# Routing's heads on VectorE, query weights in own buffers, x ahead of the second weight, attention's mask as one product

## The chip, the core and the metric

The kernel runs on one core of a Trainium2 chip. The metric is the device time of one execution in microseconds, taken as the median of several; before the change it is 4402.1 us, the median of 3 runs from 4399.16 to 4411.26 us. The core's engines work side by side, each in the order of its own queue: TensorE (PE in the profile, its weight loads PEld), VectorE (DVE), ScalarE (ACT), GpSimd (POOL) and SyncE (SP), whose queue here issues most of the transfers.

## The reference

The input is one sequence of 512 tokens of width 1024. A first block of two layers does, in each layer, a gated feed-forward, a mixer of three kinds of heads (windowed attention, mLSTM, RWKV-7), a second feed-forward and a gated projection of side features. A second block has one layer: a hybrid mixer, cross-attention, and a layer of retrieved experts. The two parts that the change touches most are attention's masked scores and the experts' routing:

```python
# attention: bands of 128 queries by 256 keys, 8 query heads on 2 key heads
scores = einsum(qb, kb) * HEAD_DIM ** -0.5
scores = where(valid, scores, NEG_INF)
probs = softmax(concatenate([scores, sink]))[..., :-1]

# routing of the experts: 8 heads, two key halves of 128 keys each
q = (t @ wq).reshape(ntok, 8, 2, 128)
sc = einsum('thpd,hpkd->thpk', q, subkeys)
s1, i1 = top_k(sc[:, :, 0], 16)
s2, i2 = top_k(sc[:, :, 1], 16)
cand = s1[..., :, None] + s2[..., None, :]
best, pos = top_k(cand, 16)          # over the 256 sums
idx = i1[pos // 16] * 128 + i2[pos % 16]
gate = softmax(best)
# then: out = sum over the 128 chosen experts of gate * gelu(u[idx] . t) * v[idx]
```

## The kernel before

The activations lie feature-major: eight tiles of 128 features by 512 tokens. Every large product is done in three products of fp32r halves (`mm3`): a weight tile of 128 output features is loaded by SP (`st`, 2 buffers), cast to its high half on ScalarE (`wh`, line 186) and its low half is the difference (`wl`, line 187), on the engine that `wl_eng` names, VectorE unless a caller sets GpSimd. `wh` and `wl` have three buffers each (`HEAD`). `lin_fm` runs over the output tiles: each takes 8 blocks of 128 inputs, so 24 products of 512 columns, into a PSUM bank, and then calls `evac`. With `head` = 3 it computes the first three output tiles together, half of the tokens at a time.

*The order.* The program is written as one stream; a planner then fills each engine's queue by the order of the program and by the times that it expects, and sets the semaphores. An engine serves its queue in order.

*The start.* `start` loads the vectors `V`, then the eight tiles of x one after the other, with the first three weights of the feed-forward in between, and splits each x tile into halves on ScalarE and VectorE (lines 220 and 221). The norm's scale (`bcast_R`, sums `ssum`) is applied at `evac`.

*Attention.* For each of 4 blocks of 128 queries and each pair of heads, two PSUM banks hold the scores of the two key heads (256 keys for each of two query heads). A product of the identity with the mask in bf16 adds the mask behind each score product: four score products and four mask products. The generator is stepped between other tiles of the mixer.

*Routing* (`peer_route`, from about 3010 to 3366 us). The 16 query tiles (two for each head) go through `lin_fm`. `evac` copies a tile to `q`, and `lists` for the tile before it computes the scores against 128 keys and, on VectorE, takes the best 16 of each of 4 token blocks in five instructions (`top16`, lines 1663 to 1667). After each second tile, `head` adds the two lists into a grid of 136 candidates (GpSimd, `cd`), takes its best 16 (VectorE), splits the position into row and column, and finds the two keys: a comparison of the position with 0..15 on VectorE (`eq`, line 1721), a product with the key numbers on GpSimd (line 1722), a sum on VectorE (line 1723), once for each half. The gate's differences, scaling and last product are on GpSimd, its Exp on ScalarE. After each head, `early(5)` computes five of the experts' projections of 384 tokens (`peer_z`, 24 products of 384 columns; their `wl` on GpSimd, evacuated on VectorE, line 1603), and `gather(2)` does two products of the gathered rows of token block 0 (line 1797). After routing come the gate matrices (`peer_gates`, to about 3570 us, with 22 to 24 more projections) and the experts (`peer_experts`, to about 4330 us). Products of routing use four banks in turn for query tiles and projections, and four for scores.

## Time and profile before

| | |
|---|---|
| median of 3 runs | 4402.1 us |
| the profiled execution | 4405.5 us |
| its span | 4403.7 us |
| TensorE busy | 4137.3 us (94%) |
| VectorE, ScalarE, GpSimd busy | 2627.9 (60%), 1609.7 (37%), 852.8 us (19%) |
| granted TensorE clock, mean | 0.964 |
| traffic, mean | 143 GB/s |

Times are counted from the span's start. A row of busy time by stretch gives the stretch, its length, then for PE, PEld, DVE, ACT and POOL the busy time and the number of instructions, then the granted clock of TensorE as a share of 2.4 GHz, the share of the 16 DMA engines that is busy, and GB/s. A row of the timeline gives start, duration, engine, line, operation, tiles written and read, and in brackets the engine's idle time just before with what ended it. A row of a group gives line, engine, operation, tiles, sizes and count, then busy time in all, mean duration in ns, and the idle time before. Busy times of a pipelined engine overlap, so the starts tell more than the durations.

### The profile page before, as it was taken

What the parts mean: (1) busy time and instruction counts of PE and PEld (TensorE: products, weight loads), DVE (VectorE), ACT (ScalarE), POOL (GpSimd) and SP (SyncE); (2) the same over time, 40 slices, a digit from 0 to 9 for tenths busy, and PEclk for the clock granted to TensorE, in tenths of its full rate; (3) what the DMA queues carried; (4) which work ended last, traced back from release to release, by engine and by line L of the source; (5) the groups of instructions that cost most, each with busy time, mean ns of one, the idle gap of its engine ahead of it and who ended that gap; (6) DMA issues with size and microseconds to landing.
All of it is one profiled execution on the core that took longest, in us unless ns stands there. A gap on an engine that the chain in (4) does not pass through costs nothing. (4 is left out here: it accounts for less than half of the span.)

```text
span 4403.7 us, 56669 instructions
## 1 busy us (share of the span) xinstructions
PE 4137.3 (94%) x21835; PEld 3513.9 (80%) x21835; DVE 2627.9 (60%) x4873; ACT 1609.7 (37%) x2522; POOL 852.8 (19%) x755
## 2 busy tenths in 40 slices
PE   8999999999999999999999889899887889999998
PEld 7887687888888876878888677788777878888887
DVE  5435555643564345656434666636667878777876
ACT  3223423422443234324323543433334743333332
POOL 0002210100110012111001242104564124333331
PEclk9999989999999998989999899999898999999999
DMA  3233101323332341003223311435345689889985
GB/s 126 98 94 123 48 15 48 120 99 96 121 120 96 96 135 44 25 30 120 96 97 124 108 53 34 143 107 178 135 149 182 253 323 334 303 312 318 317 311 183
DMA packets 234815, 629.18 MB, mean 143 GB/s; under 512 B 26800, under 2 KB 93488, under 8 KB 230192
## 3 DMA queue, kind: packets, MB, share of 16 engines
q1 hardware_dynamic: 195232, 464.58, 30.8%
q0 software_dynamic: 38736, 159.93, 10.1%
q8 instruction: 171, 2.80, 0.2%
q10 hardware_dynamic: 576, 1.05, 0.1%
q14 instruction: 100, 0.82, 0.1%
HBM read 562.54 MB, written 62.91 MB: 142 GB/s over the span
## 5 line engine op out<-in xcount | busy, mean ns | idle before, releaser
L196 PE MATMUL ps_ps<-xh,wl 128*128 128x512 f32 (+2 forms) x3568 | 1307.3, 367 | 53.6 <-DVE wl L187 53.6
L196 PE MATMUL ps_ps<-xh,wh 128*128 128x512 f32 (+2 forms) x3568 | 1306.7, 368 | 32.6 <-ACT wh L186 11.9
L196 PE MATMUL ps_ps<-xl,wh 128*128 128x512 f32 (+2 forms) x3568 | 1314.2, 369 | 24.2 <-DVE xl L343 23.8
L186 ACT CAST wh<-st 128x1024 fp32r<-128x1024 f32 (+1 forms) x560 | 580.0, 1038 | 1405.2 <-PE ps_ps L196 962.3
L187 DVE TENSOR_TENSOR wl<-st,wh 128x1024 fp32r<-128x1024 f32 (+1 forms) x496 | 607.2, 1225 | 440.4 <-ACT wh L186 439.3
L196 PEld LDWEIGHTS ps_ps<-xh,wl 128*128 128x128 f32 x3568 | 689.0, 193 | 146.9 <-DVE wl L187 59.9
L196 PEld LDWEIGHTS ps_ps<-xl,wh 128*128 128x128 f32 x3568 | 688.1, 193 | 116.1 <-DVE xl L343 35.2
L196 PEld LDWEIGHTS ps_ps<-xh,wh 128*128 128x128 f32 x3568 | 686.4, 193 | 117.9 <-ACT wh L186 13.4
L442 DVE TENSOR_TENSOR gu<-ps_ps,R 128x512 f32<-128x512 f32 x176 | 121.0, 691 | 447.6 <-PE ps_ps L196 446.8
L348 POOL TENSOR_TENSOR y<-y,x 128x256 f32<-128x256 f32 x64 | 54.8, 856 | 1693.7 <-DVE y L347 1511.6
L196 PE MATMUL ps_ps<-mh,wl 128*128 128x512 f32 (+1 forms) x920 | 327.8, 356 | 2.5 <-DVE wl L187 2.5
L196 PE MATMUL ps_po<-vh,ah 128*128 128x512 f32 x768 | 303.2, 397 | 28.6 <-ACT ah L1845 21.8
L196 PE MATMUL ps_ps<-mh,wh 128*128 128x512 f32 (+1 forms) x920 | 327.4, 356 | 1.2 <-DVE kf L1518 0.9
L196 PE MATMUL ps_po<-vh,al 128*128 128x512 f32 x768 | 304.6, 397 | 4.5 <-DVE al L1846 4.4
L196 PE MATMUL ps_po<-vl,ah 128*128 128x512 f32 x768 | 303.2, 395 | 0.4 <-DVE vl L1852 0.4
L196 PE MATMUL ps_ps<-ml,wh 128*128 128x512 f32 (+1 forms) x792 | 289.4, 365 | 0.0
L187 POOL TENSOR_TENSOR wl<-st,wh 128x1024 fp32r<-128x1024 f32 x64 | 155.9, 2437 | 248.3 <-ACT wh L186 226.2
L1786 POOL DMA_INDIRECT rows<-in_pv_dram,idx x128 | 174.8, 1366 | 121.8 <-DVE acc L1809 114.1
L196 PEld LDWEIGHTS ps_ps<-mh,wl 128*128 128x128 f32 x920 | 174.9, 190 | 26.7 <-DVE wl L187 2.7
L196 PEld LDWEIGHTS ps_po<-vh,ah 128*128 128x128 f32 x768 | 146.4, 191 | 62.0 <-ACT ah L1845 26.2
L196 PEld LDWEIGHTS ps_ps<-mh,wh 128*128 128x128 f32 x920 | 174.8, 190 | 25.7 <-DVE kf L1518 1.1
L196 PEld LDWEIGHTS ps_po<-vh,al 128*128 128x128 f32 x768 | 146.1, 190 | 41.9 <-DVE al L1846 11.6
(699 smaller groups left out, 6047.2 us busy)
## 6 DMA issues: line engine op xcount, KB each, us to landing
st<-in_pu_dram SPq DMA_DIRECT2D x128, 512.0 KB
vst<-in_pv_dram SPq DMA_DIRECT2D x128, 512.0 KB
st<-in_w1i_dram SPq DMA_DIRECT2D x88, 512.0 KB
st<-in_w2i_dram SPq DMA_DIRECT2D x88, 512.0 KB
G<-gst POOLq DMA_DIRECT2D x12, 2048.0 KB
gt<-G SPq DMA_DIRECT2D x384, 64.0 KB
st<-in_wmf_dram SPq DMA_DIRECT2D x44, 512.0 KB
xd<-y SPq DMA_DIRECT2D x20, 1024.0 KB
```

Of the source, the lines that this page charges most:

```text
L186: nc.scalar.copy(out=wh[:, :n], in_=st[:, :n])
L187: self.wl_eng.tensor_sub(wl[:, :n], st[:, :n], wh[:, :n].bitcast(F32))
L196: i = self.nc.tensor.matmul(out, lhsT=lhsT, rhs=rhs, start=start, stop=stop)
L348: nc.gpsimd.tensor_add(y[k + 1], y[k + 1], self.xin[k + 1][:, c])
L442: nc.vector.tensor_mul(t, psum, R)
L1786: self.nc.gpsimd.indirect_dma_start(out=t, out_offset=None, in_=self.d["pur" if w == "u" else "pvr"], in_offset=bass.IndirectOffsetOnAxis( ...
```

## The change

- `__init__`: `V` is loaded from ScalarE's queue; a memset on GpSimd and one Square on ScalarE follow it.
- `start` takes one weight and loads it after the first x tile; the other seven x tiles follow. The first feed-forward of layer 0 has `head=0`, so it takes its output tiles one by one; its first tile uses the weight that `start` loaded.
- `attention`: for each bank one product of the identity with the mask, repeated for the two query heads, opens the accumulation; the four score products follow, and the second closes it.
- `peer_route`: `head` does on VectorE what was on GpSimd, save the last gate product and the copy of block 0's gates; the key numbers are copied to fp16 on ScalarE; both halves' comparison and product are each one instruction over 2048 fp16 values (pairs innermost), summed by three halvings and a last sum. The gate's steps stand ahead of the keys.
- Query tiles 2 to 15 have a staging buffer of their own (`qst`, one) and halves of their own (`qh`, `ql`, two each), loaded two tiles ahead. `early` runs after each tile, three after an even one and two after an odd one; the lists of the last tile are called behind the loop.

```diff
@@ -126,3 +126,6 @@
         self.V = V[:, :NV]
-        nc.sync.dma_start(out=self.V, in_=d["V"])
+        nc.scalar.dma_start(out=self.V, in_=d["V"])
+
+        nc.gpsimd.memset(V[:, NV:NV + 1], 0.0)
+        nc.scalar.activation(V[:, NV + 1:NV + 2], V[:, NV:NV + 1], AF.Square)
         self.sump.tile([P, XPAD], F32, name="pad")
@@ -288,4 +291,4 @@
             nc.sync.dma_start(out=x[k], in_=self.xd[k // 4][:, (k % 4) * T:(k % 4 + 1) * T])
-            if k % 2 == 0 and k // 2 < len(w):
-                self.held.append(self.load_w(w[k // 2], KD, P))
+            if k == 0:
+                self.held.append(self.load_w(w, KD, P))
             self.pre_split(x[k], k, gain)
@@ -396,3 +399,3 @@
             for src, k0, nk in wsrc(m):
-                wh, wl = self.load_w(src, nk, P)
+                wh, wl = self.held.pop(0) if self.held else self.load_w(src, nk, P)
                 for k in range(nk):
@@ -431,3 +434,3 @@
-    def ffn(self, w_in, w_out, post_gain, next_gain):
+    def ffn(self, w_in, w_out, post_gain, next_gain, head=None):
         nc, tc = self.nc, self.tc
@@ -449,3 +452,3 @@
-            self.lin_fm(lambda m: [(w_in[m], 0, KD)], list(range(2 * FT)), self.xs, evac, "ps", head=HEAD)
+            self.lin_fm(lambda m: [(w_in[m], 0, KD)], list(range(2 * FT)), self.xs, evac, "ps", head=HEAD if head is None else head)
             self.post_begin()
@@ -1101,7 +1104,7 @@
                 ks = slice((b - 1 + k0) * P, (b + 1) * P)
+                for e in range(2):
+                    self.mm(sc[e][:, :, k0 * P:], self.id16, bc(self.m16[:, k0 * P:256].unsqueeze(1), [P, 2, 256 - k0 * P]), True, False)
                 for g in range(2):
                     for e, o in enumerate(rows):
-                        self.mm(sc[e][:, g, k0 * P:], QT[j0 + g][o, sl], KT[o, ks], True, False)
-                    for e in range(2):
-                        self.mm(sc[e][:, g, k0 * P:], self.id16, self.m16[:, k0 * P:256], False, True)
+                        self.mm(sc[e][:, g, k0 * P:], QT[j0 + g][o, sl], KT[o, ks], False, g == 1)
                 mx = small("mx", [2, 2])
@@ -1613,3 +1616,3 @@
             with tc.tile_pool(name="pr", bufs=1) as rp:
-                self.peer_route(rp, iota, sl, early, yk)
+                self.peer_route(rp, im, sl, early, yk)
             with tc.tile_pool(name="pg", bufs=1, reuse_waits="tile") as gp:
@@ -1651,3 +1654,3 @@
-    def peer_route(self, pool, iota, slots, early, yk):
+    def peer_route(self, pool, im, slots, early, yk):
@@ -1659,3 +1662,4 @@
         si = pool.tile([P, NB, 16, 16], U32, name="si")
-        tok = [pool.tile([P, NB, P], F32, name=f"tok{i}") for i in range(3)]
+        tk = pool.tile([P, 3, NB, P], F32, name="tok")
+        tok = [tk[:, i, :, :] for i in range(3)]
         t = lambda nm, sh, dt=F32, bufs=2: pool.tile([P] + sh, dt, tag=nm, name=nm, bufs=bufs)
@@ -1674,4 +1678,2 @@
                 lists(*late.pop(0))
-            if m == 15:
-                lists(*late.pop(0))
@@ -1683,3 +1685,3 @@
                 self.mm(pc[:, b, :], q[:, b * P:(b + 1) * P], sk[:, m, :])
-            sc = t("sc", [NB, P], bufs=3)
+            sc = t("sc", [NB, P])
             for b in range(NB):
@@ -1688,6 +1690,6 @@
                 head(m // 2)
+            self.wl_eng = nc.gpsimd
+            early(3 - m % 2)
+            self.wl_eng = nc.vector
             if m % 2:
-                self.wl_eng = nc.gpsimd
-                early(5)
-                self.wl_eng = nc.vector
                 self.gather(2, self.anchor)
@@ -1696,8 +1698,9 @@
             s1, s2 = sv[:, :, 2 * h, :], sv[:, :, 2 * h + 1, :]
+            sf = t("sf", [2, NB, 16, 2], F16)
+            for w in range(2):
+                nc.scalar.copy(out=sf[:, w, :, :, :], in_=bc(si[:, :, 2 * h + w, :].unsqueeze(3), [P, NB, 16, 2]))
             cd = t("cd", [NB, 136])
             grid = [P, NB, 8, 16]
-            nc.gpsimd.tensor_copy(out=cd[:, :, 0:128].rearrange("p b (i j) -> p b i j", j=16), in_=bc(s2.unsqueeze(2), grid))
-            c4 = cd[:, :, 0:128].rearrange("p b (i j) -> p b i j", j=16)
-            nc.gpsimd.tensor_add(c4, c4, bc(s1[:, :, 0:8].unsqueeze(3), grid))
-            nc.gpsimd.tensor_add(cd[:, :, 128:136], s1[:, :, 8:16], bc(s2[:, :, 0:1], [P, NB, 8]))
+            nc.vector.tensor_add(cd[:, :, 0:128].rearrange("p b (i j) -> p b i j", j=16), bc(s2.unsqueeze(2), grid), bc(s1[:, :, 0:8].unsqueeze(3), grid))
+            nc.vector.tensor_add(cd[:, :, 128:136], s1[:, :, 8:16], bc(s2[:, :, 0:1], [P, NB, 8]))
             bv, bp = t("bv", [NB, 16]), t("bp", [NB, 16], U32)
@@ -1706,28 +1709,32 @@
             hs = slice(h * 16, (h + 1) * 16)
-            hi, lo, k1, k2 = (t(n, [NB, 16]) for n in ("hi", "lo", "k1", "k2"))
-            for o, op, c in ((hi, ALU.logical_shift_right, 4), (lo, ALU.bitwise_and, 15)):
-                pi = t("pi", [NB, 16], U32)
-                nc.vector.tensor_scalar(pi, bp, c, None, op0=op)
-                nc.gpsimd.tensor_copy(out=o, in_=pi)
-
-            nc.vector.scalar_tensor_tensor(k2, hi, 8.0, lo, op0=ALU.is_ge, op1=ALU.mult)
-            nc.vector.tensor_add(k1, hi, k2)
-            nc.vector.tensor_sub(k2, lo, k2)
-            full = [P, NB, 16, 16]
-            for w, key in enumerate((k1, k2)):
-                sf = t("sf", [NB, 16])
-                nc.gpsimd.tensor_copy(out=sf, in_=si[:, :, 2 * h + w, :])
-                eq = t("eq", [NB, 16, 16])
-                nc.vector.tensor_tensor(eq, bc(key.unsqueeze(3), full), bc(iota[:, 0:16].unsqueeze(1).unsqueeze(1), full), op=ALU.is_equal)
-                nc.gpsimd.tensor_mul(eq, eq, bc(sf.unsqueeze(2), full))
-                nc.vector.tensor_reduce(tok[w][:, :, hs], eq, axis=AX.X, op=ALU.add)
             g = tok[2][:, :, hs]
-            nc.gpsimd.tensor_sub(g, bv, bc(bv[:, :, 0:1], [P, NB, 16]))
-            nc.gpsimd.tensor_mul(g, g, bc(self.r.unsqueeze(2), [P, NB, 16]))
+            nc.vector.tensor_sub(g, bv, bc(bv[:, :, 0:1], [P, NB, 16]))
+            nc.vector.tensor_mul(g, g, bc(self.r.unsqueeze(2), [P, NB, 16]))
             nc.scalar.activation(g, g, AF.Exp)
+            pi, hl = t("pi", [2, NB, 16], U32), t("hl", [2, NB, 16])
+            for w, (op, c) in enumerate(((ALU.logical_shift_right, 4), (ALU.bitwise_and, 15))):
+                nc.vector.tensor_scalar(pi[:, w, :, :], bp, c, None, op0=op)
+            nc.vector.tensor_copy(out=hl, in_=pi)
+            hi, lo = hl[:, 0, :, :], hl[:, 1, :, :]
+
+            k, over = t("k", [2, NB, 16], F16), t("over", [NB, 16])
+            nc.vector.scalar_tensor_tensor(over, hi, 8.0, lo, op0=ALU.is_ge, op1=ALU.mult)
+            nc.vector.tensor_add(k[:, 0, :, :], hi, over)
+            nc.vector.tensor_sub(k[:, 1, :, :], lo, over)
+
+            eq = t("eq", [64, 16, 2], F16, 1)
+            nc.vector.tensor_tensor(eq, bc(k.rearrange("p w b (r two) -> p (w b r) two", two=2).unsqueeze(2), [P, 64, 16, 2]),
+                                    bc(im[:, 0:16, :].unsqueeze(1), [P, 64, 16, 2]), op=ALU.is_equal)
+            e4 = eq.rearrange("p (a r) j two -> p a r (j two)", r=8)
+            nc.vector.tensor_mul(e4, e4, bc(sf.rearrange("p w b j two -> p (w b) (j two)").unsqueeze(2), [P, 8, 8, 32]))
+            for n in (8, 4, 2):
+                nc.vector.tensor_add(eq[:, :, 0:n, :], eq[:, :, 0:n, :], eq[:, :, n:2 * n, :])
+            for w in range(2):
+                x = eq[:, 32 * w:32 * w + 32, :, :].rearrange("p (b r) j two -> p b r j two", r=8)
+                nc.vector.tensor_add(tok[w][:, :, hs].rearrange("p b (r two) -> p b r two", two=2), x[:, :, :, 0, :], x[:, :, :, 1, :])
             sm = t("sm", [NB])
             nc.vector.tensor_reduce(sm, g, axis=AX.X, op=ALU.add)
-            self.anchor = nc.vector.reciprocal(sm, sm)
+            nc.vector.reciprocal(sm, sm)
+            self.anchor = nc.vector.scalar_tensor_tensor(self.idx[:, hs], tok[1][:, 0, hs], float(P), tok[0][:, 0, hs], op0=ALU.mult, op1=ALU.add)
             nc.gpsimd.tensor_mul(g, g, bc(sm.unsqueeze(2), [P, NB, 16]))
-            nc.vector.scalar_tensor_tensor(self.idx[:, hs], tok[1][:, 0, hs], float(P), tok[0][:, 0, hs], op0=ALU.mult, op1=ALU.add)
             nc.gpsimd.tensor_copy(out=self.gate0[:, hs], in_=tok[2][:, 0, hs])
@@ -1736,3 +1743,22 @@
-        self.lin_fm(lambda m: [(d["wpq"][m], 0, KD)], list(range(16)), self.xs, evac, "ps", head=2, between=lambda: self.token_major(yk))
+        def qw(m):
+
+            st = t("qst", [1024], F32, 1)
+            qh, ql = (t(n, [1024], F32R) for n in ("qh", "ql"))
+            nc.sync.dma_start(out=st, in_=d["wpq"][m])
+            nc.scalar.copy(out=qh, in_=st)
+            nc.vector.tensor_sub(ql, st, qh.bitcast(F32))
+            return [x.rearrange("p (a b) -> p a b", b=P) for x in (qh, ql)]
+
+        self.lin_fm(lambda m: [(d["wpq"][m], 0, KD)], [0, 1], self.xs, evac, "ps", head=2, between=lambda: self.token_major(yk))
+        w = [qw(2), qw(3)]
+        for m in range(2, 16):
+            qh, ql = w.pop(0)
+            pt = self.ps([P, T], "ps")
+            for k in range(KD):
+                self.mm3(pt, (qh[:, k, :], ql[:, k, :]), self.xs[k], k == 0, k == KD - 1)
+            if m + 2 < 16:
+                w.append(qw(m + 2))
+            evac(m, pt)
+        lists(*late.pop(0))
         early(2)
@@ -2019,3 +2045,3 @@
         k = K(ctx, tc, d)
-        k.start("ffn1_pre0", [d["w1i"][0][m] for m in range(HEAD)])
+        k.start("ffn1_pre0", d["w1i"][0][0])
         with tc.high_priority(offset=-0):
@@ -2023,3 +2049,3 @@
         for l in range(2):
-            k.ffn(d["w1i"][l], d["w1o"][l], f"ffn1_post{l}", f"mix_pre{l}")
+            k.ffn(d["w1i"][l], d["w1o"][l], f"ffn1_post{l}", f"mix_pre{l}", head=HEAD if l else 0)
             k.mix(l, f"ffn2_pre{l}")
```

## Rows read from the trace of the kernel before

**Rows 1.** Busy time by stage: feed-forward and expert stretch (columns in the section above)
```profile
60.00:230.00 170.00, 170.00 (x752) 140.81 (x751) 77.61 (x93) 50.54 (x62) 0.00 (x0) 1.00 0.29 99
3570.00:4328.00 758.00, 724.94 (x3404) 627.17 (x3404) 596.37 (x805) 258.61 (x362) 277.38 (x215) 0.98 0.91 318
```

**Rows 2.** Waits of PE from 3024 to 3366 us: total, times, longest
```profile
PE ps_ps L196 <- DVE wl L187: 48.3, 8, 6.8
PE ps_ps L196 <- DVE sm L1730: 9.0, 3, 3.2
```

**Rows 3.** Timeline of PE around one routing period
```profile
3098.98 0.79 PE L196 MATMUL ps_ps<-xh,wl 128*128 128x512 f32 x1 [6.76 <-DVE wl L187]
3141.90 0.79 PE L196 MATMUL ps_ps<-xh,wl 128*128 128x512 f32 x1 [6.76 <-DVE wl L187]
```

**Rows 4.** Busy time in that period and in its first stretch
```profile
3098.90:3142.00 43.10, 36.26 (x185) 33.53 (x185) 27.82 (x121) 13.45 (x17) 25.03 (x21) 0.90 0.38 134
3098.90:3104.00 5.10, 5.02 (x12) 3.95 (x13) 5.10 (x28) 1.09 (x2) 0.94 (x1) 0.50 0.88 297
```

**Rows 5.** Timeline of DVE in the same period
```profile
3133.68 1.22 DVE L1723 TENSOR_REDUCE tok<-eq 128x64 f32<-128x1024 f32 x1 [2.29 <-POOL eq L1722]
3140.63 1.22 DVE L187 TENSOR_TENSOR wl<-st,wh 128x1024 fp32r<-128x1024 f32 x1
```

**Rows 6.** Instruction groups of DVE from 3108 to 3151 us: busy, mean ns
```profile
L1603 DVE TENSOR_TENSOR zs<-ps_ps,R 128x384 f32<-128x384 f32 x5 | 2.7, 541 | 0.0
L1723 DVE TENSOR_REDUCE tok<-eq 128x64 f32<-128x1024 f32 x2 | 2.4, 1220 | 3.4 <-POOL eq L1722 3.4
L1721 DVE TENSOR_TENSOR eq<-k,iota 128x1024 f32<-128x1024 f32 x2 | 2.4, 1218 | 0.0
L1663 DVE MAX8 sv<-ps_rt 128x8 f32<-128x128 f32 x8 | 2.3, 288 | 7.5 <-PE ps_rt L196 7.5
L1714 DVE TENSOR_TENSOR k<-hi,k 128x64 f32<-128x64 f32 x1 | 0.2, 226 | 0.0
```

**Rows 7.** Instruction groups of DVE in the gate stage, 3396 to 3530 us
```profile
L1761 DVE TENSOR_TENSOR o<-im,slot 128x2048 f16<-128x2048 f16 x18 | 21.9, 1217 | 0.0
```

**Rows 8.** Timeline of POOL and DVE near 3062 us; one line's durations (min/median/max ns)
```profile
3061.97 2.39 POOL L187 TENSOR_TENSOR wl<-st,wh 128x1024 fp32r<-128x1024 f32 x1
3063.20 2.25 DVE L1797 CUSTOM_DVE_ANT_0 row<-row,htok 128x1024 f32<-128x1024 f32 x1 [3.30 <-DMA row<-in_pur_dram,idx]
L1797 DVE CUSTOM_DVE_ANT_0 row<-row,htok x11: 1211/1217/2254, 3058.7 to 3356.7; 128x1024 f32<-128x1024 f32 x11
```

**Rows 9.** Timeline of PE behind the last routing head
```profile
3360.40 0.69 PE L196 MATMUL ps_ps<-xh,wl 128*128 128x384 f32 x1 [5.46 <-DVE wl L187]
```

**Rows 10.** Timeline of ACT and PE at the start
```profile
5.03 1.28 ACT L220 ACT_TABLE_LOAD   x1 [5.03 <-DMA x<-in_xT_dram]
8.03 0.58 PE L196 MATMUL ps_ps<-xh,wh 128*128 128x256 f32 x1 [8.03 <-ACT wh L186]
23.91 1.05 PE L196 MATMUL ps_pr<-io,ssum 128*128 128x1 f32 x8 [2.75 <-DVE ssum L425]
41.15 0.50 PE L196 MATMUL ps_ps<-xh,wl 128*128 128x512 f32 x1 [0.19 <-DVE wl L187]
```

**Rows 11.** Busy time, clock and DMA of two stretches of the start
```profile
5.00:10.00 5.00, 1.50 (x5) 1.05 (x5) 2.74 (x4) 4.96 (x7) 0.00 (x0) 1.00 0.95 341
25.00:30.00 5.00, 5.00 (x32) 5.00 (x32) 2.65 (x27) 0.70 (x3) 1.26 (x8) 0.66 0.00 2
```

**Rows 12.** Instruction groups of PE over the span: mask products
```profile
L196 PE MATMUL ps_at<-m,id 128*128 128x256 bf16 x48 | 11.6, 297 | 0.0
```

**Rows 13.** Timeline of POOL in the period of rows 4
```profile
3122.35 2.40 POOL L187 TENSOR_TENSOR wl<-st,wh 128x1024 fp32r<-128x1024 f32 x1
3138.12 0.29 POOL L1731 TENSOR_TENSOR tok<-tok,sm 128x64 f32<-128x64 f32 x1 [2.16 <-DVE sm L1730]
3138.48 1.13 POOL L1733 COPY gate<-tok 128x16 f32<-128x16 f32 x1
```

## The prediction

> **What bounds the kernel now.** TensorE is the busiest engine over the span, so I read busy time by stage first, then, where TensorE stops, whom it waited for. In the feed-forward stretch it is busy for 170 of 170 us at full clock: 752 products of 512 columns, 0.226 us each. In the expert stretch it is busy 725 of 758 us with the DMA engines at 0.91 [rows 1]. Neither has room, and the diff does not touch them.
>
> Routing has room. Between 3024 and 3366 us TensorE waits 48.3 us in 8 waits for VectorE's low-half subtraction `wl`, and 9.0 us in 3 waits for the heads' end on VectorE [rows 2]. The stalls recur: one ends at 3098.98, the next at 3141.90, a period of 42.9 us for two query tiles and five expert projections [rows 3]. In one period TensorE is busy 36.26 of 43.10 us, and for the first 5.10 us behind the stall its clock is granted at 0.50, the lower of its two levels (1.2 GHz) [rows 4]. So a period is 6.8 us of stall, 5.1 x 0.5 = 2.6 us lost to the clock, and 33.7 us of work; I use 33.8, and 42.9 - 33.8 = 9.1 us is the most a period can give back. The other engines are busy there for 27.8 us (VectorE), 25.0 (GpSimd) and 13.5 (ScalarE).
>
> Why VectorE is late: its queue holds the query tile's `wl` behind the head. Inside the head it waits 2.29 us for GpSimd's product `eq`, and the wanted `wl` starts only at 3140.63, right after the head and two gather products [rows 5].
>
> **Part 1, the routing heads.** Per head VectorE loses two comparisons and two reductions: 2 x 1.218 + 2 x 1.220 = 4.9 us [rows 6]. It gains:
> - the two grid sums: 512 values lie between 384 (0.541) and 1024 (1.218), estimate 0.6, the small one 0.2; two products on 64 values at 0.226; one cast of 128 values, about 0.25 [rows 6];
> - one comparison and one product over 2048 fp16 values. The gate stage does this very form, pairs innermost, in 1.217 us [rows 7]: 2.4;
> - three halving sums over 1024, 512 and 256 fp16 values. The trace has none; bounds 3 x 0.226 = 0.7 and 3 x 1.217 = 3.7. They shrink from half of that row's size, so I take 1.2, near the lower end;
> - two last sums on 64 values: 0.45.
>
> Together 0.8 + 0.45 + 0.25 + 2.4 + 1.2 + 0.45 = 5.6, net +0.7: VectorE goes from 27.8 to 28.5 us a period (31.0 at the upper bound), below 33.8. ScalarE gains two small copies (0.2 to 0.6 us each) on 13.5. GpSimd loses both `eq` products, the grid, the casts and two gate steps, and keeps five `wl` of 2.4 us, two gathers and the last gate product. So VectorE inside a head now waits only for TensorE's scores and ScalarE's copies and Exp.
>
> **Part 2, query weights in own buffers.** The work is the same: one load, one cast, one subtraction a tile. What moves is when: tile m + 2 is cast once tile m has left TensorE, and is needed 28 us later (a period without one tile, 33.8 - 24 x 0.226). VectorE's backlog is at most one head: twenty top-16 instructions of 0.29 [rows 6], 5.8 us, then the same on the grid and some 7 us of sums (5.6 and the small ones that stay), 13. So the wait for `wl` should go. Cost: the staging buffer is single, so a load on SP's queue may stand until the previous tile's subtraction is done, with the projections' loads behind it. Bounds 0 and the 6.8 us it replaces; I take 0, nearest to the 28 us of slack; the other end is a rival below. The projections go out 3 and 2 between tiles instead of 5 together: same count, no cost.
>
> **What is late next.** VectorE, 28.5 of 33.8 us, serves in order, and it empties the projections' banks too. GpSimd beside it adds to that. A gather product on VectorE that reads two tensors from SBUF started at 3063.20 during a GpSimd `wl` (3061.97 to 3064.36) and took 2.25 us instead of 1.22 [rows 8]: it stood until `wl` had ended. The head's new work is of that two-input kind; with the gathers and own subtractions it comes to about 13 of 34 us. Five `wl` x 13/34 = 1.9 meetings, mean loss half of 2.4 us: 2 to 3 us a period, bounds 0 and 5 x 2.4 = 12. I take 3, nearer to the median gather product (1.217): VectorE 31.5 of 33.8. So full an engine cannot always be in time; I leave a third of the old loss, 3.1 us, in the period: 36.9. Seven periods lie between the first head and the eighth: 7 x (42.9 - 36.9) = **-42** (at most -64; a loss is a rival below).
>
> The Trainium skill, "SBUF — State Buffer", section "Who interferes with whom", says that a VectorE instruction with two SBUF inputs and a GpSimd instruction that reads SBUF exclude each other, and the second to start blocks fully. The 2.25 us agree. By that rule which of them starts first sets the price, so it can reach the upper bound above, and heads on VectorE are less free than its busy share says.
>
> **Tail of routing.** Behind the last scores there were seven projections (5 + 2) of 24 x 0.17 us (0.226 x 384/512), 29 us; now four, 17 us. The last head needs 5.8 + 13 us plus Exp and the transposes: 3 us come out uncovered. Against that, the tail had its own stall of 5.46 us for a `wl` [rows 9]. Bounds -8 (that stall and its slow clock) and +12 (three projections' cover); I take **+3**.
>
> **Part 3, the start.** TensorE starts at 8.03, because ScalarE loads its table for 1.28 us only when x has come (5.03). It waits 2.75 us for the norm's sums, and the third product of the fourth tile starts at 41.15 [rows 10]. In full-width products that is number 75: 74 x 0.226 = 16.7 us at full clock, so 24.4 us were lost. After: the table is loaded while x is under way and x leads SP's queue, start about 6.7; half clock over the first 6.8 us of work, as I read it from the same start: +3.4; 16.7 of work: 26.8. All of x now goes ahead of the second weight; 3.2 MB behind the first 5 us at 341 GB/s [rows 11] put that weight at 14.4 us, cast and split by 16.7, against the first tile's end at 15.5: +1.2. The wait for the sums with its clock loss (0.66 over the next 5 us [rows 11]) costs 0 to 4.5, I take 3: 31. One weight at a time also leaves two of three weight buffers free for the next tiles. **-10** (bounds -14 and 0).
>
> **Part 4, attention's mask.** 64 products of the mask become 32 of twice the width, ahead of the scores. The row gives 297 ns for 256 columns [rows 12], but the columns stay; at most 32 x 0.297 = 9.5 us go, at worst a us or two is lost where the mask waits for its bank. TensorE's other waits surround this stage: **-1**.
>
> **Sum.** -42 + 3 - 10 - 1 = -50. The profiled execution took 4405.5 us (span 4403.7 and 1.8 around it), which gives 4355; it is 3.4 above the median 4402.1. From the median: **4352**.
>
> **The rivals.**
> - *The stall goes whole.* VectorE's queue keeps ahead, TensorE runs 33.8 us periods, the tail costs nothing: 4402 - 64 - 14 - 1 = 4323. For it: nothing in the head waits for GpSimd any more. Against: VectorE is over 84% busy before any blocking.
> - *GpSimd blocks VectorE at nearly every turn* (12 us): period 28.5 + 12 = 40.5, 7 x 2.4 = 17: 4402 - 17 - 10 - 1 + 3 = 4377. For it: the 2.25 us. Against: the median of the gather products is 1.217 [rows 8].
> - *The single staging buffer holds SP's queue*: a new wait as long as the old, and routing gains nothing: 4402 - 10 - 1 + 3 = 4394.
> - *GpSimd's order turns the head into a wait; slower.* The last gate product stays on GpSimd and waits for VectorE's whole head. If the projections' `wl` stand behind it in GpSimd's queue, TensorE idles from the scores on: 18.8 us of VectorE, then about 1.4 of GpSimd's gate steps and 2.4 of `wl`: 22.6, plus 2.6 of clock: period 59, 7 x 16.1 = +113: 4402 + 113 - 8 = 4507. It makes the kernel slower from about 10 us of waiting a period. Against: today a `wl` runs at 3122.35, between the steps of a head, and the gate product follows at 3138.12 [rows 13]. For it: the order is planned from expected times, which shift with a longer VectorE head.
>
> **How the numbers follow.** Forecast 0.48 (its own range 4335 to 4370), stall gone whole 0.20, GpSimd blocking 0.15, SP's queue 0.07, slower 0.10. A measurement here tells 0.3% (13 us) from no change: the first three are faster, 0.83; the fourth lies within, 0.07; the last is slower, 0.10. The range 4316 to 4390 holds the first three and leaves out the rest.
>
> **What would show it.** Right: no recurring wait of TensorE for `wl` in routing, heads 36 to 38 us apart, granted clock there above 0.95, VectorE above 80% busy; TensorE's start near 6.7 and the fourth tile ten us earlier. Wrong: in each period a wait of TensorE of 7 us or more, for GpSimd's `wl` or for a load; sums of 2 us or more each in VectorE's head; a new gap ahead of the gates.

## The result and the profile after

The median after is 4343.32 us (4 executions, 4337.61 to 4360.9) against 4406.68 us for the kernel before on the same chip: ratio 0.9866, 95% interval 0.9844 to 0.9887. By the two medians that is 63 us less, by the ratio 59, where the sum gave 50. Nearly all of it comes from routing. The table divides every profiled execution at the starts of the norms' scales on VectorE, and ends routing where VectorE starts on the last list that routing writes (`slot`, the gates); "heads" is the mean distance of two heads' comparisons (of their first ones in e5 to e7). The kernels e1 to e12 are those of the next section; each ratio is to runs of before on the same chip (medians 4399.77 to 4410.54 us).

| kernel | time, us | ratio to before (95%) | first feed-forward ends | first mixer | routing | heads |
|---|---|---|---|---|---|---|
| before | 4406.68 | 1 | 377.8 | 366.8 | 351.6 | 42.9 |
| after | 4343.32 | 0.9866 (0.9844 to 0.9887) | 376.1 | 383.6 | 287.5 | 33.6 |
| e1 routing part alone | 4353.12 | 0.9885 (0.985 to 0.9919) | 380.1 | 367.9 | 288.6 | 33.8 |
| e2 start alone | 4406.53 | 0.999 (0.9969 to 1.0011) | 376.3 | 372.0 | 351.9 | 42.9 |
| e3 mask alone | 4413.62 | 1.001 (0.9986 to 1.0033) | 379.3 | 366.3 | 352.7 | 43.0 |
| e4 heads alone | 4342.25 | 0.9857 (0.9826 to 0.9888) | 380.5 | 371.9 | 294.2 | 34.8 |
| e5 buffers, old head | 4427.02 | 1.0041 (1.0026 to 1.0056) | 379.4 | 366.6 | 368.1 | 45.0 |
| e6 after + 2 comparisons a head | 4381.95, once | | 375.6 | 383.6 | 307.2 | 36.4 |
| e7 after + 4 comparisons a head | 4371.49, once | | 375.9 | 367.6 | 330.9 | 39.4 |
| e8 sums later in the program | 4344.2 | 0.9851 (0.9813 to 0.9889) | 376.0 | 383.6 | 287.2 | 33.6 |
| e9 sums forced later | 4347.98 | 0.9879 (0.9862 to 0.9895) | 375.6 | 365.7 | 287.3 | 33.6 |
| e10 query's low half on GpSimd | 4330.2 | 0.984 (0.9823 to 0.9856) | 375.9 | 371.9 | 286.4 | 33.6 |
| e11 heads + buffers | 4372.18 | 0.994 (0.9923 to 0.9957) | 379.2 | 369.7 | 319.1 | 38.1 |
| e12 heads + spread | 4385.6 | 0.9963 (0.995 to 0.9976) | 379.3 | 370.7 | 330.6 | 39.8 |

The profiled execution of after is the longest of its four: span 4359.1 us, 44.6 less than before's. Routing gives 64.1 of that; the first mixer takes 16.8 back.

The end of routing depends on the order in which its lists are written: in after the gates' list is written before the last head's keys are ready, in before and in e4 behind them. Two later marks, in us from routing's start, do not depend on that list alone:

| mark | before | after | e1 | e4 | e11 | e12 |
|---|---|---|---|---|---|---|
| first comparison of the gate matrices | 352.0 | 298.0 | 299.0 | 293.1 | 318.0 | 340.7 |
| end of the span | 1393.8 | 1330.3 | 1330.3 | 1334.9 | 1351.9 | 1366.7 |

To the end of the span the gain is 63.5 us, so it does not hang on where routing is taken to end.

Busy time of after in two stretches of the start, one of the first mixer and one period of routing (columns as in [rows 4]):

```profile
15.00:20.00 5.00, 0.39 (x2) 0.00 (x0) 4.96 (x6) 3.61 (x4) 3.47 (x3) 0.84 0.01 6
20.00:25.00 5.00, 3.56 (x13) 2.84 (x14) 3.45 (x30) 0.23 (x1) 0.53 (x1) 0.50 0.00 0
...
690.00:710.00 20.00, 20.00 (x65) 16.62 (x66) 9.26 (x28) 3.07 (x6) 2.65 (x3) 0.55 0.05 20
...
3146.40:3179.40 33.00, 33.00 (x183) 31.04 (x182) 30.53 (x128) 13.68 (x20) 16.67 (x9) 1.00 0.51 174
```

The last row answers [rows 4]: TensorE is busy 33.00 of 33.00 us at full clock, where it was busy 36.26 of 43.10 at 0.90; VectorE goes from 27.82 to 30.53 us, GpSimd from 25.03 to 16.67. Over the seven periods from the first head's comparison to the eighth's TensorE is busy 231.3 of 235.3 us, and all that it lacks lies in the last; VectorE is busy 218.8, so 93%. The wait that recurred [rows 2] is left once, behind the last head. TensorE's waits in after from 3040 to 3340 us:

```profile
PE ps_ps L199 <- DVE wl L190: 3.7, 1, 3.7
PE ps_g L199 <- DVE p L1790: 1.9, 1, 1.9
PE ps_g L199 <- ACT gst L1798: 1.1, 2, 0.6
PE ps_rt L215 <- POOL tok L1739: 1.0, 1, 1.0
PE ps_g L199 <- DVE p L1789: 1.0, 1, 1.0
PE ps_ps L199 <- POOL wl L190: 0.2, 1, 0.2
```

VectorE's queue in after, at the start and in routing (it answers [rows 5]; lines have moved by three and more):

```profile
15.62 1.89 DVE L505 CAST M<-mf 128x1280 uint8<-128x1280 f32 x1
17.43 1.74 DVE L278 TENSOR_TENSOR ssum<-ssum,sqx 128x512 f32<-128x512 f32 x1
19.43 0.68 DVE L428 TENSOR_TENSOR ssum<-ssum,ssum 128x512 f32<-128x512 f32 x1
24.23 1.22 DVE L190 TENSOR_TENSOR wl<-st,wh 128x1024 fp32r<-128x1024 f32 x1
...
3082.96 0.27 DVE L1731 TENSOR_TENSOR eq<-eq 128x256 f16<-128x256 f16 x1
...
3146.43 1.23 DVE L1726 TENSOR_TENSOR eq<-k,im 128x2048 f16<-128x2048 f16 x1
3147.71 1.22 DVE L1729 TENSOR_TENSOR eq<-eq,sf 128x2048 f16<-128x2048 f16 x1
3149.11 0.68 DVE L1731 TENSOR_TENSOR eq<-eq 128x1024 f16<-128x1024 f16 x1
3150.95 0.41 DVE L1731 TENSOR_TENSOR eq<-eq 128x512 f16<-128x512 f16 x1
3151.56 2.21 DVE L1731 TENSOR_TENSOR eq<-eq 128x256 f16<-128x256 f16 x1
...
3164.44 2.17 DVE L1750 TENSOR_TENSOR ql<-qst,qh 128x1024 fp32r<-128x1024 f32 x1 [2.23 <-ACT qh L1749]
```

GpSimd's in the same period (it answers [rows 13]):

```profile
3149.16 0.79 POOL L1739 TENSOR_TENSOR tok<-tok,sm 128x64 f32<-128x64 f32 x1 [6.15 <-DVE sm L1737]
...
3151.05 2.56 POOL L190 TENSOR_TENSOR wl<-st,wh 128x1024 fp32r<-128x1024 f32 x1
...
3163.12 2.40 POOL L190 TENSOR_TENSOR wl<-st,wh 128x1024 fp32r<-128x1024 f32 x1 [1.36 <-ACT wh L189]
```

Read the two together: nothing in the head waits for GpSimd, but the sum of 256 values takes 2.21 us where it takes 0.27 without a `wl` beside it, and ends 0.16 us after GpSimd's `wl` does (3153.77 against 3153.61); `ql` takes 2.17 beside the next one. The last product of the gate waits 6.15 us for VectorE, with the gates' copy and then a `wl` behind it, the order that the fourth rival feared, and TensorE stays busy throughout.

The Trainium skill, "SBUF — State Buffer", section "Who interferes with whom", says that a VectorE instruction with two SBUF inputs contends with a GpSimd instruction that reads SBUF, and calls the port pair that they share an exclusive lock; the 2.21 against 0.27 us agree.

TensorE at the start and behind the last head (it answers [rows 10] and [rows 9]):

```profile
7.54 0.79 PE L199 MATMUL ps_ps<-xh,wh 128*128 128x512 f32 x1 [7.54 <-ACT wh L189]
20.17 1.87 PE L199 MATMUL ps_pr<-io,ssum 128*128 128x1 f32 x8 [4.78 <-DVE ssum L428]
24.37 1.86 PE L199 MATMUL ps_pr<-io,rsy 128*128 128x128 f32 x7 [1.27 <-DVE rsy L239]
...
3312.85 0.69 PE L199 MATMUL ps_ps<-xh,wl 128*128 128x384 f32 x1 [3.70 <-DVE wl L190]
```

It starts 0.5 us earlier, and then waits 4.78 us for the norm's sums where it waited 2.75.

### The profile page after: what moved, and what is told of

It is laid out like the page before. It is cut to its first block, busy times and chain, and to the rows that moved or that the text cites. A ratio compares the mean times of both kernels' runs of the same rounds, so it can differ in the third digit from the quotient of the medians.

```text
span 4359.1 us, 56445 instructions
## 1 busy us (share of the span) xinstructions
PE 4138.8 (95%) x21731; PEld 3522.8 (81%) x21731; DVE 2657.1 (61%) x4937; ACT 1612.0 (37%) x2539; POOL 800.9 (18%) x668
## 5 line engine op out<-in xcount | busy, mean ns | idle before, releaser
L199 PE MATMUL ps_ps<-xl,wh 128*128 128x512 f32 (+2 forms) x3432 | 1263.9, 369 | 23.8 <-DVE xl L346 23.1
L199 PE MATMUL ps_ps<-xh,wh 128*128 128x512 f32 (+2 forms) x3432 | 1259.3, 368 | 21.3 <-ACT xh L354 12.6
L199 PE MATMUL ps_ps<-xh,wl 128*128 128x512 f32 (+2 forms) x3432 | 1255.7, 367 | 7.7 <-DVE wl L190 7.4
L189 ACT CAST wh<-st 128x1024 fp32r<-128x1024 f32 (+1 forms) x546 | 565.9, 1038 | 1332.9 <-PE ps_ps L199 928.5
L190 DVE TENSOR_TENSOR wl<-st,wh 128x1024 fp32r<-128x1024 f32 (+1 forms) x482 | 592.6, 1231 | 443.7 <-ACT wh L189 441.6
L199 PEld LDWEIGHTS ps_ps<-xl,wh 128*128 128x128 f32 x3432 | 660.9, 193 | 111.6 <-DVE xl L346 34.7
L199 PEld LDWEIGHTS ps_ps<-xh,wh 128*128 128x128 f32 x3432 | 659.1, 193 | 102.2 <-ACT xh L354 13.9
L199 PEld LDWEIGHTS ps_ps<-xh,wl 128*128 128x128 f32 x3432 | 660.9, 193 | 95.0 <-DVE wl L190 10.9
L199 PE MATMUL ps_po<-vh,ah 128*128 128x512 f32 x768 | 304.2, 398 | 31.5 <-ACT ah L1871 24.6
L1812 POOL DMA_INDIRECT rows<-in_pv_dram,idx x128 | 186.9, 1460 | 114.0 <-DVE acc L1835 106.4
```

The source lines that it names most:

```text
L189: nc.scalar.copy(out=wh[:, :n], in_=st[:, :n])
L190: self.wl_eng.tensor_sub(wl[:, :n], st[:, :n], wh[:, :n].bitcast(F32))
L199: i = self.nc.tensor.matmul(out, lhsT=lhsT, rhs=rhs, start=start, stop=stop)
L1812: self.nc.gpsimd.indirect_dma_start(out=t, out_offset=None, in_=self.d["pur" if w == "u" else "pvr"], in_offset=bass.IndirectOffsetOnAxis( ...
```

## The experiments

**The parts one by one.** e1 to e3 are the kernel before with one part of the diff each: its hunks in `peer` and `peer_route`; those in the set-up, `start`, `lin_fm`, `ffn` and `program`; that in `attention`.

> Routing's change alone (heads on VectorE, query weights in own buffers, projections spread 3 and 2); start and mask as before. Theory A (routing carries the gain): TensorE has no wait for a weight's low half in routing, heads about 33.6 us apart instead of 42.9, 60 to 68 us less than before, so about 4342 us. Theory B (the start and the mask give a fifth of it, as forecast): 50 to 55 us less.

> The start's change alone. Theory A (the start's gain was lost to the norm's sums: the first tile ends early and TensorE then waits for them at the lower clock): the first feed-forward ends 1 to 3 us earlier than before, time within 3 us of before. Theory B (the forecast's -10, and the lost part of it came from the other edits): the first feed-forward ends 8 to 12 us earlier.

> Attention's mask alone. Theory A (the longer first mixer in the changed kernel's profile was that execution's clock): time within 5 us of before, the first mixer 363 to 370 us between its norm and the next as before. Theory B (the mask's new order makes TensorE fall to its lower clock in the first mixer): 15 to 20 us slower, with the first mixer near 384 us and its mean clock near 0.89 instead of 0.94.

Routing alone brings 63.0 us of routing time, the start 1.5 us and the mask nothing that shows. By the traces that is theory A in all three: in e1 the heads are 33.8 us apart and one wait for VectorE's low half is left (3.9 us, behind the last head). The times do not decide it: e1 is 57 us below before by the medians and 51 by the ratio, between A and B, and an effect of 1 us as forecast for the mask is far below what they tell. That e2 ends as its theory A said does not show A's cause, the sums; e9 below tests that. The mask did become what the diff says. Its products in after:

```profile
L199 PE MATMUL ps_at<-m,id 128*128 128x512 bf16 x24 | 7.5, 382 | 0.0
L199 PE MATMUL ps_at<-m,id 128*128 128x256 bf16 x8 | 1.6, 278 | 0.0
```

These stand for the 48 of 256 columns and 11.6 us of [rows 12] and for 16 of the 48 of 128 columns, of which 32 are left. The time of e3 is 1.001 of before.

**Which part of routing.** Heads alone (against after; start and mask as before), and buffers without the new heads (excerpts):

```diff
# e4: the new head; lin_fm over all 16 tiles, early(5) behind each second one
-        w = [qw(2), qw(3)]
-        for m in range(2, 16):
+        self.lin_fm(lambda m: [(d["wpq"][m], 0, KD)], list(range(16)), ...)
# e5: the kernel before, with qw() and its loop, old head, early(5); and
-                eq = t("eq", [NB, 16, 16])
+                eq = t("eq", [NB, 16, 16], bufs=1)
```

> Only the heads on VectorE; query weights in the shared buffers as before, five projections together behind each head. Theory A (the stall was the query's low half behind a head that waited for GpSimd; without these waits most of it goes): the wait of 6.8 us shrinks to 1 to 3 us a period, 35 to 55 us less than before. Theory B (the own buffers matter most, since the query's low half still stands behind the head in VectorE's queue): the wait stays at 4 us or more a period, less than 25 us gained.

> Only the query weights' own buffers, two tiles ahead; heads split between VectorE and GpSimd as before (the comparison's tile with one buffer instead of two), five projections together. Theory A (two edits, one wait: the low half no longer stands behind the head, so the buffers alone remove the stall too): routing's stretch 290 to 305 us instead of 351.6, 45 us or more gained. Theory B (the head through GpSimd delays whatever follows it on VectorE, now the evacuation of the projections): TensorE still waits 4 us or more a period, less than 25 us gained.

e4, a period of heads, and its waits for `wl` (PE, 3030 to 3340 us):

```profile
3100.00:3133.00 33.00, 33.00 (x183) 31.08 (x182) 29.53 (x125) 13.28 (x19) 13.81 (x9) 1.00 0.51 174
```

```profile
PE ps_ps L196 <- DVE wl L187: 4.0, 3, 2.1
```

The heads alone give 57.4 of the 64.1 us, more than theory A's 35 to 55, and a period in the middle is already full. e5 is slower than before, which neither theory foresaw: in it the wait is not gone but stands at another place. TensorE's waits in e5 (3060 to 3380 us), then one of them, then ScalarE ahead of it:

```profile
PE ps_rt L196 <- ACT q L1671: 50.9, 6, 10.4
```

```profile
3120.83 2.07 PE L196 MATMUL ps_rt<-sk,q 128*128 128x128 f32 x8 [7.48 <-ACT q L1671]
```

```profile
3117.89 0.52 ACT L1604 ACTIVATE zs<-zs 128x384 f32<-128x384 f32 x1 [10.68 <-DVE zs L1603]
3118.32 1.03 ACT L186 CAST wh<-st 128x1024 fp32r<-128x1024 f32 x1
3119.26 1.04 ACT L1740 CAST qh<-qst 128x1024 fp32r<-128x1024 f32 x1
3120.20 0.57 ACT L1671 COPY q<-ps_ps 128x512 f32<-128x512 f32 x1
```

The copy `q` that the scores need stands in ScalarE's queue behind a projection's Gelu, which waits 10.68 us for VectorE to empty the projection, and VectorE is in the old head. But e5 is not the buffers alone. The two comparisons of a head share one buffer in it, where before has two. The second now waits for the first half's sum, and in five of the eight heads it takes over 6 us, beside two `wl` of GpSimd. One of the five, on VectorE and on GpSimd:

```profile
3106.57 6.24 DVE L1719 TENSOR_TENSOR eq<-k,iota 128x1024 f32<-128x1024 f32 x1
```

```profile
3106.99 4.73 POOL L187 TENSOR_TENSOR wl<-st,wh 128x1024 fp32r<-128x1024 f32 x2
```

It takes 6.24 us where it took 1.22 [rows 6], and from the first comparison to the last key's sum the head takes 17.1 us (3100.26 to 3117.40) where before took 8.2. So how much of the 16.5 us is the buffers' is not shown by e5. That TensorE stands for whichever product of a late VectorE is wanted next fits both kernels; what the buffers do with the head kept the same, e11 shows beside e4.

**The other two corners.** Heads with buffers, projections five together; and heads with the spread, query weights in the shared buffers:

```diff
# e11: e1 with
-            early(3 - m % 2)
             if m % 2:
+                early(5)
# e12: e1 with lin_fm over all 16 tiles in place of qw() and its loop
```

> The kernel before, with the routing heads on VectorE and the query weights in buffers of their own, but the five projections still together behind each odd tile and not three and two between tiles; start and mask as before. e4_heads (heads alone) had routing at 294 us, with 34.8 us between heads; e1_route (heads, buffers and spread) 288.6 us and 33.75. Theory A (the heads do nearly all; the spread gives the last 6 us, because it lets VectorE empty projections between the heads): routing 292 to 297, time 4342 to 4355. Rival B (the buffers give it): 286 to 290, the same time within what can be told. Rival C (the buffers alone made routing 16 us longer in e5_bufs, and do so here without the spread): routing 300 to 312, time 4355 to 4370.

> The kernel before, with the routing heads on VectorE and the projections spread three and two between the query tiles, but the query weights in the shared buffers as before: the fourth corner beside e4_heads (neither: routing 294.2 us, 34.8 us between heads), e11_headsbufs (buffers alone: 319.1, 38.1) and e1_route (both: 288.6, 33.75). Theory A (the spread is worth something only where the buffers have brought the query weights forward, and repairs that; without them there is little to repair): routing 288 to 295, TensorE's waits in routing under 6 us in all, time 4338 to 4350. Rival B (the spread alone is what takes routing from 294 to 288, the buffers are worth nothing): 285 to 289, time 4335 to 4343. Rival C (the spread needs the buffers: a query tile's weight in the shared buffers stands behind the projections' weights between the tiles, and TensorE waits for it): a wait for a weight at each tile, routing 300 to 330, time 4350 to 4385.

Both are rival C, at or beyond its upper end. With routing at 294.2 us for heads alone, buffers make it 319.1, the spread 330.6, both 288.6: added to the heads each by itself costs 25 and 36 us (17 and 32 to the end of the span). Together they cost nothing, but that they give anything is not shown: by the table's end of routing they gain 5.6 us over the heads, to the end of the span 4.6, to the start of the gate matrices they lose 5.9, and the median of e4, 4342.25, is the lower one (e1 4353.12, after 4343.32; the intervals overlap). PE's waits in e11 (3030 to 3360 us) and in e12 (3030 to 3380 us):

```profile
PE ps_rt L196 <- ACT q L1672: 18.6, 6, 6.9
PE ps_ps L196 <- POOL wl L187: 7.2, 5, 1.8
```

```profile
PE ps_ps L196 <- DVE wl L187: 21.2, 5, 8.2
PE ps_ps L196 <- POOL wl L187: 9.5, 4, 4.3
```

In e11 it is the wait of e5, for `q`, and here beside e4, which has the same head. In e12 it is the wait of before, for a query tile's `wl`; ScalarE, VectorE and TensorE around one of them:

```profile
3116.61 0.53 ACT L1604 ACTIVATE zs<-zs 128x384 f32<-128x384 f32 x1 [6.93 <-DVE zs L1603]
3117.04 1.03 ACT L186 CAST wh<-st 128x1024 fp32r<-128x1024 f32 x1
```

```profile
3120.05 1.52 DVE L187 TENSOR_TENSOR wl<-st,wh 128x1024 fp32r<-128x1024 f32 x1
```

```profile
3121.62 0.80 PE L196 MATMUL ps_ps<-xh,wl 128*128 128x512 f32 x1 [4.13 <-DVE wl L187]
```

The weight's cast stands behind a Gelu that waits for VectorE, and its low half starts 2.0 us after the cast has ended (3118.07), behind other work in VectorE's queue; in after the query weight is by its code cast a tile earlier. Why e4, with neither, is free of both waits, no run took apart.

**How full VectorE may be.** e6 and e7 repeat the head's comparison into the same tile two and four times more; e10 takes work away:

```diff
# e6 (2), e7 (4)
+            for _ in range(2):
+                nc.vector.tensor_tensor(eq, bc(k...), bc(im...), op=ALU.is_equal)
# e10
-            nc.vector.tensor_sub(ql, st, qh.bitcast(F32))
+            nc.gpsimd.tensor_sub(ql, st, qh.bitcast(F32))
```

> The changed kernel with the comparison of 2048 values done three times instead of once in each head: 2.4 us more of VectorE a period. Theory A (TensorE sets the period and VectorE has slack until its work fills 33.6 us): the heads stay 33.4 to 34.4 us apart. Theory B (each us on a VectorE this full shows in part, as the forecast's 3.1 us assumed): 35 us or more.

> The same with five comparisons: 4.9 us more of VectorE a period, busy 31 + 5 = 36 of 33.6. Theory A: VectorE now sets the period, 35.5 to 37 us, with waits of TensorE for VectorE. Theory B: 37 us or more, with TensorE's clock falling behind each wait.

> The kernel after, with the low half of the two query tiles of a period subtracted by GpSimd in place of VectorE: some 2.4 us of VectorE's period go, GpSimd gets some 4.8 us more on 16.7. Theory A (after the change TensorE has no idle time left in routing, 33.0 of 33.0 us, so that VectorE's load matters only when it grows): routing stays at 286 to 290 us, heads 33.5 to 33.8 us apart, time as after within 8 us. Rival B (VectorE still sets part of the period): routing 275 to 282, time 4330 to 4337. Rival C (the low half on GpSimd stands behind the head's gate product, which waits 6 us for VectorE, and TensorE waits for it): a wait of TensorE for ql in every period, routing 300 to 330, time 4357 to 4385.

TensorE's waits for the emptying of the projections, in e6 and in e7 (3050 to 3360 us):

```profile
PE ps_ps L199 <- DVE zs L1606: 12.2, 5, 4.6
```

```profile
PE ps_ps L199 <- DVE zs L1606: 30.2, 7, 8.7
```

Two comparisons are 2.4 us a head, and heads come 2.8 us later; four are 4.9 and cost 5.8. That is theory B in both runs (in e7 the granted clock is 0.94 over its seven periods): work added to VectorE shows in full already at 2.4 us. Taken away, it shows nothing in routing. A period of e10:

```profile
3127.90:3161.50 33.60, 33.60 (x186) 31.64 (x186) 29.57 (x127) 14.19 (x21) 20.48 (x11) 1.00 0.51 171
```

VectorE has 29.57 us in it, TensorE is full, heads stay 33.6 us apart: theory A. So in after TensorE bounds routing, with VectorE just in time. e10's time is the lowest of all and lies where rival B put it, but its routing is only 1.1 us shorter than that of after, and the two ratios' intervals overlap. Of the two profiled executions e10's is 17.5 us shorter, and 17.2 of these lie ahead of routing, where the kernels do not differ (routing starts at 3011.6 in e10, at 3028.8 in after); why the other executions of e10 are shorter still is not shown.

**The start.** e8 put the sums of the norm behind three tiles in the program, e9 forced that order on the engines:

```diff
-            _, R = self.bcast_R()
+            R = None if head == 0 else self.bcast_R()[1]
             def evac(m, psum):
+                if R is None:
+                    pend.append((m, psum))
+                    if len(pend) == 3:
+                        R = self.bcast_R()[1]   # e9: behind the third tile's wl and products
+                        for p in pend:
+                            evac(*p)
+                    return
```

> The changed kernel with the first norm's sums and scale put behind the first three output tiles of the first feed-forward; those three wait in their banks for the scale. Theory A (TensorE stood 4.8 + 1.3 us for the sums that its queue held ahead of the second tile, and ran at the lower clock for 8 us behind that): no wait of TensorE between 15 and 22 us beyond 2 us, the first feed-forward ends 7 to 11 us earlier than in the changed kernel, near 367 us. Theory B (the second weight is late anyway): it ends less than 3 us earlier.

> The kernel after, with the first norm's sums and scale kept, by an order written out by hand, behind the first three output tiles on TensorE, and the VectorE addition of the sums behind the third tile's low-half subtraction; the three tiles are emptied after that. It does what e8_deferR was to do and did not. Theory A (the start gave 2 us and not 10 because TensorE stands 4.8 us behind the first tile for the sums of the squares, and runs slower for it): no such wait between 15 and 20 us, granted clock above 0.8 from 15 us on, the first feed-forward ends 7 to 11 us earlier than after (365 to 369 us against 376), time near 4335. Rival B (the start is bound by the second and third weight, cast and split; the sums merely fill that wait): the wait comes back for a weight's low half, the first feed-forward ends at 374 to 378, time as after, 4343. Rival C (the time lost is given back by emptying the three tiles together): the wait goes, but a later one takes its place while the tiles are emptied, the end at 371 to 375.

e8 missed its aim: the planner left the sums behind the first tile, with 5.06 us of wait. e9 took that wait away, and another came in its place; TensorE in e9, then VectorE, then ScalarE:

```profile
22.49 0.79 PE L199 MATMUL ps_ps<-xh,wl 128*128 128x512 f32 x1 [5.83 <-DVE wl L190]
```

```profile
15.11 1.90 DVE L517 CAST M<-mf 128x1280 uint8<-128x1280 f32 x1
16.93 1.74 DVE L278 TENSOR_TENSOR ssum<-ssum,sqx 128x512 f32<-128x512 f32 x1
...
21.21 1.22 DVE L190 TENSOR_TENSOR wl<-st,wh 128x1024 fp32r<-128x1024 f32 x1
```

```profile
14.84 1.03 ACT L189 CAST wh<-st 128x1024 fp32r<-128x1024 f32 x1
```

Rival B holds: the first feed-forward ends at 375.6. The second weight is cast at 15.87, and its low half begins 5.3 us later; until then VectorE's queue holds the masks' cast (`M`), a sum and the rotary tables (18.79 to 21.21) ahead of it. The sums of the norm merely filled the same time. That an order with the low half ahead of these tables would gain the time back is argued; no run has it.

## Why the prediction was right, and where it was not

- *What bounds it, and the work in a period*: right. 33.8 us of work forecast; a period in which TensorE never stops took 33.0, the mean of seven 33.6.
- *VectorE's load*: right. Forecast 31.5 of 33.8 us, measured 30.53 of 33.0. The two large fp16 operations take 1.23 and 1.22 (2.4 forecast), the three halving sums 0.68 + 0.41 + 0.27 = 1.36 where nothing blocks them (1.2). GpSimd's blocking costs 2.21 - 0.27 = 1.9 on the sum and 2.17 - 1.22 = 0.95 on `ql`, 2.9 us where 3 were taken; in six of the seven periods it is 2.7 to 4.0, in the last nothing.
- *The step that failed*: "So full an engine cannot always be in time; I leave a third of the old loss, 3.1 us, in the period: 36.9." Heads are 33.6 us apart, so 7 x 3.3 = 23 us more went. The rival "the stall goes whole" is what routing did. An engine that is busy 93% of the time was in time at every turn but the last head's (3.7 us); e6 shows that 2.4 us more would have made the step nearly true (36.4). Of the prediction's signs of being wrong one did come, a sum of 2 us or more in the head (2.21), and no wait with it.
- *The parts of the edit*: the prediction gave the end of the wait to the query weights' buffers and the spread "no cost". The runs give it to the heads, 57.4 us alone; the buffers added to them cost 25. The queue that it did not price is ScalarE's: it counted "two small copies", not that `q` stands behind a Gelu there. That the two edits came together spared the sum their 25 and 36 us, and that was luck: the prediction had no step for it.
- *Tail*: +3 forecast. Routing is 64.1 us shorter and seven periods 7 x (42.88 - 33.61) = 64.9, so about +1, and by the end of the span the same (63.5). To SP's queue, the third rival, no wait of TensorE in after leads, and to GpSimd's, the fourth, one of 0.2 us.
- *Start*: -10 forecast. In the profiled execution the first feed-forward ends 1.6 us earlier; over all profiles here the seven with the new start have it at 375.6 to 376.3, the seven with the old one at 377.8 to 380.5, 3.4 us between the means. The term that failed is "cast and split by 16.7": cast it was by then, split at 25.45 (24.23 + 1.22), and at 22.43 in e9. The wait for the sums, 4.78 us, lay beyond its upper bound, and the clock fell to 0.50; by e9 the low half would have kept TensorE waiting without it. The first tile ended at 15.4, as forecast (15.5), by two errors that cancel: it started 0.8 us later than the 6.7 taken, and lost 2.4 us to the clock where 3.4 were taken.
- *Mask*: -1 forecast, none seen.

The errors of routing (25 us too little) and start (7 too much) partly cancel: the sum gave -50, and -63 came by the medians. That the time lies in the forecast's own range of 4335 to 4370 owes something to that.

*The first mixer stays open.* Its 383.6 us in after, e6 and e8 go with a low clock: 0.55 from 690 to 710 us, with TensorE busy throughout. The same microseconds of e7, further on in the program:

```profile
690.00:710.00 20.00, 20.00 (x95) 16.07 (x95) 15.04 (x40) 6.58 (x10) 3.59 (x3) 1.00 0.15 55
```

e7 is the same program up to routing and took 367.6 us, so the longer form is not fixed by the program. But three of six profiles with start and mask had it, and none of the eight others; that these two parts make it more frequent is not excluded. Routing starts at 2992 to 3029 us in those six (mean 3013.2) and at 3006 to 3016 in the eight (mean 3010.8): up to there start and mask together bring nothing that shows. e6 took longer than e7 though it has less to do, and that lies here too: its routing starts 27 us later.

## What to carry to other kernels

When one in-order engine is late for everybody, price the shortening of its longest chain first: here moving work *onto* the late engine took it out of waits for another and gave nearly all of the gain, while buffers added to that, without the spread, brought a wait at the next queue. Before counting an edit as free, follow the wanted instruction back through every queue that it stands in, ScalarE's too. A busy share of 93% is not by itself a stall, but adding a known operation twice tells in one run how much room is left. And an edit made only to fit an experiment in, such as one buffer for two, can be its main effect: look at the durations of what it touches.

## What had not been expected of the hardware

- Which of two engines is blocked does not follow from the starts in the trace alone. In after the sum at 3150.95 starts 0.10 us ahead of GpSimd's `wl` and runs free in 0.41, and the `wl` takes 2.56 instead of 2.40. In e11 VectorE's subtraction starts 0.14 us ahead, and takes 3.62 us instead of 1.22; in e5 the comparison above starts 0.42 us ahead and takes 6.24. The Trainium skill, "SBUF — State Buffer", section "Who interferes with whom", lets the order of issue decide who blocks; the 3.62 and 6.24 us do not follow that order by the starts that the trace shows. VectorE and GpSimd in e11:

```profile
3104.62 3.62 DVE L1747 TENSOR_TENSOR ql<-qst,qh 128x1024 fp32r<-128x1024 f32 x1 [1.52 <-ACT qh L1746]
```

```profile
3104.76 2.38 POOL L187 TENSOR_TENSOR wl<-st,wh 128x1024 fp32r<-128x1024 f32 x1
```

- TensorE's clock was granted at 0.55, so mostly at the lower of its two levels (1.2 GHz), in 20 us in which the trace has it busy without a gap, and the stretch before was no emptier; in the same microseconds of e7, which is further on in the program there, at 1.00.
